# An encoder block on one core: gate weights' loads, the squares and 1/rms of h2, and the loads of the last activations

## The chip, the cores and the metric

The kernel runs on one core of a Trainium2 chip. The metric is the device time of one execution in microseconds (us); lower is better. Five engines work side by side, each with a queue of its own that it works through in order: TensorE (PE in the profile; its weight loads PEld) does the matrix products, VectorE (DVE) and ScalarE (ACT) the elementwise work, GpSimd (POOL) some elementwise work and DMAs that add to what is there, SyncE (SP) issues most DMAs. The three runs of the kernel before took 2572.34 to 2573.46 us, with a median of 2573.32 us.

## The reference

One layer of an encoder for 512 tokens of 2048 numbers each, all in float32:

```
u = rms_norm(h, mix_pre_g)
[q|k|v|conv_a|conv_b|gate_attn|gate_conv] = u @ w_in
y_attn = neighbourhood_attention(q, k, v, rpb) @ w_attn_o
y_conv = conformer_conv(conv_a, conv_b) @ w_conv_o
merged = sigmoid(gate_attn) * y_attn + sigmoid(gate_conv) * y_conv
h = h + rms_norm(merged @ w_out, mix_post_g)            # this is h2
u = rms_norm(h, ffn_pre_g)
f = (silu(u @ w_gate) * (u @ w_up)) @ w_down            # 5632 hidden units
h = h + rms_norm(f, ffn_post_g)
```

`rms_norm` divides every token by the root of the mean of its squares over the 2048 numbers and multiplies with a gain for each number.

## The kernel before

All tensors lie with the features on the 128 partitions and the 512 tokens in the free dimension, so that 2048 features are 16 tiles of 128x512 (`KT` = 16, `HT` = 8). Float32 precision is reached by splitting each operand into a rounded part and the rest (`split`, `wchunk`, tiles `..h` and `..l`, `whi` and `wlo`): a product of a 128x128 block of weights with a tile takes three matmuls. The rounded part is made on ScalarE, the rest on VectorE. The large products (the gates, the two FFN matrices) are done in a Strassen-like scheme of seven products (`strassen`, L219 and on).

Four pools matter. `slot` has 66 buffers of 128x512 and holds nearly everything. `raw` (five buffers of 128x1024) holds weights as they are loaded, `whi` and `wlo` (three each) their split parts. PSUM has four banks under `mm` (`bank`) and four under `at` (`abank`).

The order of the work on each engine is set when the program is built: a planner takes the instructions by their place in the written order, gives out buffers as they come free, and lets a later instruction go ahead of an earlier one that is not ready by its own estimate of times. `keep_in_program_order` (a pin) makes an instruction wait for its place in the written order on its engine. `load_in_order` is a pinned load on SP's queue. On the chip each engine then follows its fixed order and waits for semaphores.

The stages are: the input norm and the convolution branch; v; q and k with the attention, head by head; the gates; the two output projections of the branches; `w_out`, and h2; the FFN's first matrix (gate and up), and its second (`w_dn`); the last norm. The change touches four places.

**The first gate products (L546 to L595).** Eight chunks of gate weights (`raw[c]`, from `w_gg`) and eight pairs of tiles of the normalized input (`uf[c]`, from `u_d`), which are turned into the Strassen operands, go through the same five `raw` buffers. The loads are issued in the order gate 0, un 0, gate 1, un 1, gate 2, un 2 and so on, all pinned, and are written ahead of the chunk's products.

**h2, its squares and 1/rms (L692 to L744).** Every tile of h2 is made on VectorE (`h2`, L698), split, written to `h_d`, and squared on ScalarE. The squares of the 16 tiles have to be added. Tiles 0, 1 and 2 start three sums (`acc`); the squares of tiles 3 to 13 are added to them by DMAs of GpSimd (L723), tile i to sum i % 3; tiles 14 and 15 stay by themselves. `folded` (L328) then adds these five tiles up on VectorE (L331), `rstd` (L291) sums over the partitions with short matmuls against a column of ones (L299, two passes for each block of 128 tokens: eight instructions for one tile), and VectorE and GpSimd make 1/rms of it. `by_column` (L312) spreads it over the partitions with matmuls (L316), and r3 is copied from there (L734). The steps are put between products that do not need them: the `gemm` at L729 has four chunks, and calls one of the functions in `between` behind each. 1/rms stands behind the second, r3 behind the third. With r3 the FFN's first products are finished (L740 to L744), and all operands of the next stage are made (L754 and on).

**The loads of the last activations (L870 to L908).** The second FFN matrix is done in three parts: four tiles of the hidden units, 16 tiles by the Strassen scheme, in pairs of outputs `o` = 0, 2, .. 14, and the last 24 (`acts`, tiles 20 to 43). `load` (L791) fetches a tile with a pinned DMA on GpSimd's queue and splits it (tiles `fa..`). The first three (`EARLY`) are written ahead of the pair `o` = 14 and five more (`MORE`) behind its products. Behind every pair but the last, `added` (L866) multiplies the pair's two outputs on GpSimd and adds them to `y_d` with a DMA, all pinned.

**The last norm (L915 to L975).** The last two outputs (14 and 15) are made in two halves of 256 tokens, A and B, so that the first half's norm can be made while the second half's products run. The squares of outputs 0 to 13 are summed in `acc[0]`; `sq` holds those of 14 and 15. In half A both are added to `acc[0]` on VectorE (L331), in half B only output 14's, and output 15's goes into `rstd` as a second tile. The half's 1/rms stands behind the first chunk of half B.

## Time and profile before

| | |
|---|---|
| median of three runs | 2573.32 us |
| the profiled execution | 2572.55 us |
| its span, from the first to the last instruction | 2570.8 us |
| granted TensorE clock, mean | 0.992 |
| busy: TensorE, VectorE, ScalarE, GpSimd | 98%, 73%, 44%, 13% |
| waits of TensorE over 2 us in total, by line | 8 |

The profile lists for every engine what it executed and, from the semaphores, what ended each wait. "PE f L195 <- DVE u_15l L704: 2.3, 1, 2.3" reads: TensorE, at line 195, waited once, for 2.3 us, until VectorE had written `u_15l` at line 704. In a timeline the columns are start, duration, engine, line, operation and tiles, and in brackets the idle time ahead of the instruction and what ended it. In a table of stretches the columns are the length, the busy time of TensorE, its weight loads, VectorE, ScalarE and GpSimd (with the number of instructions), the granted TensorE clock as a share, the busy share of the DMA engines, and GB/s. Durations of neighbouring matmuls overlap.

### The profile page before, as it was taken

What the parts mean: (1) busy time and instruction counts of PE and PEld (TensorE: products, weight loads), DVE (VectorE), ACT (ScalarE), POOL (GpSimd) and SP (SyncE); (2) the same over time, 40 slices, a digit from 0 to 9 for tenths busy, and PEclk for the clock granted to TensorE, in tenths of its full rate; (3) what the DMA queues carried; (4) which work ended last, traced back from release to release, by engine and by line L of the source; (5) the groups of instructions that cost most, each with busy time, mean ns of one, the idle gap of its engine ahead of it and who ended that gap; (6) DMA issues with size and microseconds to landing.
All of it is one profiled execution on the core that took longest, in us unless ns stands there. A gap on an engine that the chain in (4) does not pass through costs nothing.

```text
span 2570.8 us, 34587 instructions
## 1 busy us (share of the span) xinstructions
PE 2517.5 (98%) x13187; PEld 2160.3 (84%) x13187; DVE 1867.3 (73%) x2406; ACT 1123.7 (44%) x1652; POOL 338.4 (13%) x384
## 2 busy tenths in 40 slices
PE   9999999999999999999999999999999999989996
PEld 7888888788888888888888888888888878878886
DVE  5999896587776664337888888788888888863335
ACT  5223333455554422225455555555555564442221
POOL 0110222210000021001001111112110102240002
PEclk9999999999999999999999999999999999999998
DMA  6246323486667445237256566666665667773334
GB/s 208 94 146 194 109 93 108 142 267 185 191 195 245 137 136 185 95 113 208 96 159 181 172 166 186 189 197 194 211 202 172 183 243 183 182 246 109 110 113 156
DMA packets 144053, 430.57 MB, mean 167 GB/s; under 512 B 16912, under 2 KB 24208, under 8 KB 143888
## 3 DMA queue, kind: packets, MB, share of 16 engines
q1 hardware_dynamic: 102144, 324.32, 38.3%
q0 software_dynamic: 22160, 69.48, 12.9%
q10 hardware_dynamic: 19584, 34.58, 3.6%
q8 instruction: 103, 1.69, 0.3%
q14 instruction: 62, 0.51, 0.1%
HBM read 371.95 MB, written 49.28 MB: 164 GB/s over the span
## 4 chain that ended last, share of the span: by engine, by line
PE 82%; DVE 10%; issue 4%; DMA 2%; ACT 1%; POOL 1%; ACTq 0%; DVEq 0%; SPq 0%; POOLq 0%
PE f L251 19%; PE f L253 10%; PE g L251 7%; PE g L253 4%; PE pd L181 3%; PE pd L177 3%; PE pd L180 3%; DVE cv L397 3%; PE d L251 3%; PE qk L181 2%; PE qk L180 2%; PE qk L177 2%; PE po L181 2%; PE po L180 2%; PE po L177 2%
## 5 line engine op out<-in xcount | busy, mean ns | idle before, releaser
L397 DVE SCALAR_TENSOR_TENSOR cv<-z,vec,cv 128x497 f32<-128x497 f32 (+14 forms) x240 | 190.9, 797 | 4.8
L132 DVE TENSOR_TENSOR wlo_wd<-raw_wd,whi_wd 128x1024 fp32r<-128x1024 f32 (+1 forms) x58 | 64.2, 1111 | 110.3 <-ACT whi_wd L131 109.0
L131 ACT CAST whi_wd<-raw_wd 128x1024 fp32r<-128x1024 f32 (+1 forms) x58 | 54.0, 934 | 166.8 <-PE pd L180 120.0
L132 DVE TENSOR_TENSOR wlo_wo<-raw_wo,whi_wo 128x1024 fp32r<-128x1024 f32 x36 | 47.5, 1319 | 106.6 <-ACT whi_wo L131 106.4
L131 ACT CAST whi_wo<-raw_wo 128x1024 fp32r<-128x1024 f32 x36 | 37.9, 1054 | 130.0 <-PE po L180 122.6
L309 POOL TENSOR_TENSOR r_r<-r_v,mhalf 128x2 f32<-128x2 f32 (+1 forms) x6 | 7.0, 1174 | 504.9 <-DVE r_v L307 454.6
L131 ACT CAST whi_y<-raw_y 128x1024 fp32r<-128x1024 f32 x32 | 33.5, 1052 | 79.4 <-PE py L180 76.2
L131 ACT CAST whi_qk<-raw_qk 128x1024 fp32r<-128x1024 f32 x32 | 33.6, 1051 | 77.1 <-PE qk L180 56.5
L132 DVE TENSOR_TENSOR wlo_qk<-raw_qk,whi_qk 128x1024 fp32r<-128x1024 f32 x32 | 40.5, 1264 | 32.2 <-ACT whi_qk L131 32.0
L132 DVE TENSOR_TENSOR wlo_y<-raw_y,whi_y 128x1024 fp32r<-128x1024 f32 x32 | 53.3, 1668 | 10.8 <-ACT whi_y L131 9.6
L650 DVE TENSOR_TENSOR gg<-py,gg 128x512 f32<-128x512 f32 x32 | 21.8, 690 | 52.6 <-PE py L181 52.6
L780 POOL TENSOR_TENSOR asum<-asum,asq 128x512 f32<-128x512 f32 x15 | 19.2, 1283 | 241.6 <-ACT asq L779 241.6
L177 PE MATMUL py<-ycl,whi_y 128*128 128x512 f32 x128 | 49.8, 389 | 0.0
L180 PE MATMUL py<-ych,whi_y 128*128 128x512 f32 x128 | 49.8, 389 | 0.0
L181 PE MATMUL py<-ych,wlo_y 128*128 128x512 f32 x128 | 49.8, 389 | 0.0
L823 ACT ACTIVATE sg<-sg 128x512 f32<-128x512 f32 x39 | 24.8, 635 | 52.2 <-DVE sg L289 52.2
L478 POOL TENSOR_TENSOR bm<-braw,msk 128x128 f32<-128x128 f32 x56 | 40.7, 760 | 16.3 <-DMA braw<-in_rpb 16.2
L804 POOL TENSOR_TENSOR an<-an,asum 128x512 f32<-128x512 f32 x16 | 26.5, 1655 | 103.6 <-DMA an<-a_d 101.7
L911 DVE TENSOR_TENSOR y<-pd,y 128x512 f32<-128x512 f32 x14 | 9.7, 692 | 41.6 <-PE pd L181 38.8
L159 PE MATMUL f<-b,whi_f 128*128 128x256 f32 x128 | 36.7, 287 | 2.2 <-DVE b L154 2.2
L868 POOL TENSOR_TENSOR ys<-ys,irow 128x512 f32<-128x512 f32 x16 | 27.1, 1692 | 77.3 <-PE d L251 41.4
L160 PE MATMUL f<-b,whi_f 128*128 128x256 f32 x128 | 36.2, 283 | 0.0
(3079 smaller groups left out, 8496.7 us busy)
## 6 DMA issues: line engine op xcount, KB each, us to landing
raw_wd<-in_w_dn SPq DMA_DIRECT2D x42, 512.0 KB, 3.7
raw_wo<-in_w_out SPq DMA_DIRECT2D x36, 512.0 KB, 3.9
raw_qk<-in_w_qk SPq DMA_DIRECT2D x32, 512.0 KB, 3.7
a_d<-sg ACTq DMA_DIRECT2D x44, 256.0 KB, 3.7
raw_v<-in_w_v SPq DMA_DIRECT2D x16, 512.0 KB, 4.5
raw_y<-in_w_ao SPq DMA_DIRECT2D x16, 512.0 KB, 4.2
gg<-g_d SPq DMA_DIRECT2D x32, 256.0 KB, 4.3
raw_y<-in_w_co SPq DMA_DIRECT2D x16, 512.0 KB, 3.6
```

What stands on the lines that cost most here:

```text
L131: cast(hi[:, s], raw[:, s])
L132: nc.vector.tensor_tensor(out=lo[:, s], in0=raw[:, s], in1=hi[:, s].bitcast(F32), op=ALU.subtract)
L159: nc.tensor.matmul(o, hi, t[:, B], start=first, stop=False, skip_group_check=True)
L160: nc.tensor.matmul(o, hi, t[:, A], start=False, stop=False, skip_group_check=True)
L177: mmul = nc.tensor.matmul(ps, hi[:, s], al, start=first, stop=False)
L180: nc.tensor.matmul(ps, hi[:, s], ah, start=False, stop=False)
L181: nc.tensor.matmul(ps, lo[:, s], ah, start=False, stop=last)
L251: nc.tensor.matmul(ps, hi[:, ws[k]], t, start=first and k == 0, stop=False, skip_group_check=True)
L253: nc.tensor.matmul(ps[:, A], lo[:, ws[k]], t[:, A], start=False, stop=last and k == HT - 1, skip_group_check=True)
L397: nc.vector.scalar_tensor_tensor(out=a[:, to], in0=z[:, fr], scalar=col(C_WDW, i * CW + w), in1=a[:, to], op0=ALU.mult, op1=ALU.add)
L478: nc.gpsimd.tensor_tensor(out=bm[:, o + i - i0], in0=raw[:, :, i * BC : (i + 1) * BC], in1=msk[:, o + i - i0, None, :].broadcast_to([P, RO ...
L868: tc.keep_in_program_order(nc.gpsimd.tensor_tensor(out=t, in0=t, in1=irow, op=ALU.mult))
```

## The change

Four places are changed.

1. The loads of the gate weights are no longer pinned, and the loads for later chunks are written behind the products of a chunk instead of ahead of them. The loads of `u_d` stay pinned.
2. The squares of h2 are added in two chains of DMAs (tiles 0 and 1, to which tiles 2 to 11 are added), and the last four (12 to 15) on VectorE as they come. `rstd` now reads three tiles and is called behind the first chunk of the `gemm`, r3 behind the second.
3. The first three of the last activations are loaded ahead of the pair `o` = 12 instead of 14.
4. In the last norm, output 15's squares of half A are no longer added to `acc[0]`; `rstd` reads them as a second tile in both halves.

```
@@ gates
     def load_gate(c):
         raw.append(wraw(f"g0_{c}"))
-        load_in_order(raw[c], w_gg[c])
+        nc.sync.dma_start(raw[c], w_gg[c])
...
     load_gate(0)
     load_un(0)
-    load_gate(1)
     for c in range(HT):
-        if c + 1 < HT:
-            load_un(c + 1)
-        if c + 2 < HT:
-            load_gate(c + 2)
         hi, lo = wchunk(w_gg[c], f"g0_{c}", raw=raw[c])
...
+        if c == 0:
+            load_gate(1)
+        if c + 1 < HT:
+            load_un(c + 1)
+        if c + 2 < HT:
+            load_gate(c + 2)
@@ h2
                 sq = slot(f"h{i}_sq")
                 nc.scalar.activation(sq, f[i], AF.Square)
-                if 3 <= i < KT - 2:
-                    nc.gpsimd.dma_start(acc[i % 3], sq, accum_op=ALU.add)
+                if i in (0, 1, KT - 4):
+                    acc.append(sq)
+                elif i < KT - 4:
+                    nc.gpsimd.dma_start(acc[i % 2], sq, accum_op=ALU.add)
                 else:
-                    acc.append(sq)
+                    folded([acc[2], sq])
...
         between=(
-            lambda: None,
-            lambda: r.append(rstd(folded(acc), D, "r3", pin=True)),
+            lambda: r.append(rstd(acc, D, "r3", pin=True)),
             lambda: nc.scalar.copy(r3, by_column(r[0], "r3", pin=True)),
@@ last activations
     for o in range(0, KT, 2):
-        if o == KT - 2:
+        if o == KT - 4:
             acts = [load(DN_S + k) for k in range(EARLY)]
@@ last norm
-            if n == 0 or q is sq[0]:
+            if q is sq[0]:
                 folded([acc[0], q], cols)
...
-            lambda: r.append(rstd(acc + sq[1:] * n, D, f"r4{n}", blocks, pin)),
+            lambda: r.append(rstd(acc + sq[1:], D, f"r4{n}", blocks, pin)),
```

## The prediction

> **What bounds the kernel now.** I read the page's first part, then TensorE's own list of waits.

> ```profile
> span 2570.8 us, 34587 instructions
> PE 2517.5 (98%) x13187; PEld 2160.3 (84%) x13187; DVE 1867.3 (73%) x2406; ACT 1123.7 (44%) x1652; POOL 338.4 (13%) x384
> ```
> ```profile
> PE r_s L299 <- DVE y_sq L331: 3.5, 1, 3.5
> PE d L251 <- ACT d14v L241: 3.4, 1, 3.4
> PE pt L518 <- DVE sc L509: 2.8, 3, 1.4
> PE f L251 <- ACT f5h L246: 2.4, 1, 2.4
> PE f L195 <- DVE u_15l L704: 2.3, 1, 2.3
> ...
> PE pd L177 <- DVE fa29l L142: 2.1, 1, 2.1
> ```

> TensorE is busy for 98% of the span, so only its few idle places can be won: 2570.8 − 2517.5 = 53.3 us, the output's tail among them. The columns of the second list are total us, times, longest us. Each part of the change has one or two of these waits beside it: `pt` stands ahead of the gate products, `u_15l` and `f5h` stand on the two sides of 1/rms of h2, `d14v` and `fa29l` go with the loads of the activations, and `r_s` at 3.5 us is the last 1/rms.

> An idle place costs more than its own length, as the granted clock shows in stretches cut to the clock's own steps:

> ```profile
> 480.86:489.71 8.85, 3.86 (x24) 3.28 (x25) 6.07 (x18) 3.89 (x11) 0.00 (x0) 1.00 0.00 0
> 489.71:493.12 3.41, 3.32 (x13) 2.92 (x12) 2.71 (x4) 1.92 (x4) 0.00 (x0) 0.50 0.00 0
> 1209.92:1213.34 3.42, 1.92 (x9) 1.26 (x7) 1.28 (x2) 0.00 (x0) 0.00 (x0) 1.00 0.05 16
> 1295.26:1302.08 6.82, 5.60 (x17) 4.83 (x18) 4.55 (x5) 4.11 (x5) 0.00 (x0) 0.50 0.71 246
> 2261.23:2268.05 6.82, 5.51 (x17) 4.74 (x18) 3.12 (x4) 4.10 (x6) 2.30 (x5) 0.50 0.99 384
> ```

> After the length of a stretch stands TensorE's busy time, and the clock is the third number from the end. The clock is 0.50 for 6.82 us after the `f5h` wait and again after the `d14v` wait, 3.4 us of work lost each time, and for 3.41 us (1.7 lost) ahead of the gate products, where TensorE had been idle for 8.85 − 3.86 = 5.0 us. A stretch with 1.92 of 3.42 us busy (third row) left it at 1.00. [...]

> **Gate weights' loads.** The four products' loads change their place in the written order and lose their pin; each `un` load stays pinned.

> ```profile
> 437.06 0.33 SPq L91 DMA_DIRECT2D raw_g<-in_w_gg  x1
> ```
> ```profile
> 480.89 0.59 ACT L141 CAST qk_1h<-qk 128x512 fp32r<-128x512 f32 x1 [10.29 <-PE qk L181]
> ...
> 490.60 1.05 ACT L131 CAST whi_g<-raw_g 128x1024 fp32r<-128x1024 f32 x1
> ```

> The first gate weights are asked for at 437.06 and cast only at 490.60, although ScalarE sat idle for 10.29 us before 480.89. The cast's place in ScalarE's queue, behind the last head's softmax, keeps TensorE without other products there; the load's landing does not. The queue gives its five buffers in the written order, and that order (gate 0, un 0, gate 1, un 1, gate 2) is the same after the change. I take 0. If the planner now places the cast ahead of the softmax, the 5.0 us ahead of the gate products and the lower clock's 1.7 go: a gain of up to 6.7. If a gate load comes late instead, I bound the loss by the longest wait of the list, 3.5. Nothing new is queued behind a load on SP: an `un` load still follows the gate load written ahead of it.

> **Squares and 1/rms of h2.** Eleven accumulating DMAs in three chains become ten in two chains (tiles 2 to 11); tiles 13 to 15 are added on VectorE. The four additions at the end go, three earlier ones come.

> ```profile
> L723 POOL DMA_DIRECT2D h_sq<-h_sq x11: 866/866/923, 1178.0 to 1201.3; - x11
> ...
> DMA to landing us min/median/max: 3.4/6.9/10.6
> ```
> ```profile
> 1212.03 1.42 DVE L331 TENSOR_TENSOR h_sq<-h_sq 128x512 f32<-128x512 f32 x2 [7.06 <-DMA h_sq<-h_sq]
> 1213.36 0.74 DVE L704 SCALAR_TENSOR_TENSOR u_15l<-f,vec,u_15h 128x512 fp32r<-128x512 f32 x1
> ```

> The first row has the accumulations' first and last issue, 1178.0 and 1201.3, the second the least, median and longest time to landing; the last one lands 10.6 us after its issue. VectorE's additions wait 7.06 us for it with `u_15l` queued behind them, and TensorE waits 2.3 us for `u_15l`. With the last tiles on VectorE no addition waits for a DMA. Three additions of 0.7 us (two take 1.42) ahead of `u_15l` are 2.1 us, against the 7.06 us of standing idle: TensorE's 2.3 us go.

> ```profile
> 1222.01 0.39 PE L177 MATMUL f<-u_0l,whi_f 128*128 128x512 f32 x1
> ...
> 1227.45 0.95 PE L299 MATMUL r_s<-ones,h_sq 128*128 128x1 f32 x8
> ...
> 1233.84 1.05 PE L316 MATMUL r_b<-ident,r_r 128*128 128x128 f32 x8
> ```
> ```profile
> 1234.93 0.59 ACT L734 COPY r<-r_b 128x512 f32<-128x512 f32 x1
> ```
> ```profile
> 1250.00:1300.00 50.00, 45.45 (x342) 43.10 (x341) 49.74 (x111) 29.18 (x66) 0.00 (x0) 0.95 0.25 79
> ```

> The sums (`r_s`) move from behind the second chunk of products (1227.45) to behind the first (1222.01), the rows (`r_b`) from behind the third to behind the second. The sums read three tiles instead of one: 24 short products for 8, 16 × 0.12 = 1.9 us more. So the first chunk ends at 1222.0 − 2.3 = 1219.7, the sums at 1222.6, the second chunk, 1227.45 − 1222.01 = 5.4 us long, at 1228.0: `r_b` comes 5.8 us ahead of 1233.84. What follows hangs on it. VectorE is busy for 49.74 of the 50 us from 1250 on, the work that starts from r3's copy at 1234.93; TensorE's `f5h` wait ends this stretch. All of it starts 5.8 us earlier, VectorE being idle before. TensorE can follow: it saves 2.3 and pays 1.9 ahead of it, and within it the waits shrink. I take −5.8. The lower clock at 1295 lasts two steps; a smaller wait should leave one of them, −1.7. Bounds: none of the move is kept (only 1.9 − 2.3 = −0.4), or it and the whole lower clock, −9.2.

> **Activations by another pair.** Loads 20 to 22 are written ahead of pair 12 instead of pair 14, on POOL's queue behind `added` of pair 10 instead of pair 12.

> ```profile
> 2235.54 0.87 POOL L869 DMA_DIRECT2D y_d<-ys  x1 [0.30 <-POOL ys L868]
> ...
> 2255.65 4.62 POOL L793 DMA_DIRECT2D ad<-a_d  x8
> ```
> ```profile
> 2235.89 1.05 ACT L246 CAST d12h<-d12q 128x1024 fp32r<-128x1024 f32 x1 [1.25 <-PE d L251]
> 2238.22 0.59 ACT L241 COPY d12v<-d 128x512 f32<-128x512 f32 x1 [1.28 <-DVE d L272]
> ...
> 2261.38 0.62 ACT L141 CAST fa20h<-ad 128x512 fp32r<-128x512 f32 x1 [4.89 <-DMA ad<-a_d]
> 2261.91 0.58 ACT L241 COPY d14v<-d 128x512 f32<-128x512 f32 x1
> ```

> The eight loads leave POOL at 2255.65, after `added` of pair 12, and the first lands 5.7 us later; its cast `fa20h` was put ahead of the copy `d14v` in ScalarE's queue, so the copy is late and TensorE waits 3.4 us. One pair earlier POOL is free at 2236.1 (its write of 2235.54 is the last of `added` of pair 10) and the load lands at about 2241.8; if the planner puts the cast at the same point of the pair, it stands ahead of `d12v` (2238.22) and that copy is 4 us late in the same way. The other five loads still leave after pair 12. So I do not count the 3.4 us as won: one such stall stays, here or there, for 0. What is won is behind it. Three activations fewer are loaded, cast and subtracted when the last products begin, and the 2.1 us for `fa29l` fall away. I take −2.1. Bounds: both pairs stall, +3.4 and its half clock +3.4; or neither does, −6.8 and −2.1.

> **The last 1/rms.** The addition of tile 15's left half goes, and `r_s` reads two tiles.

> ```profile
> 2539.95 0.42 ACT L927 ACTIVATE sq<-y 128x256 f32<-128x256 f32 x1 [1.31 <-DVE y_sq L331]
> ```
> ```profile
> 2540.40 0.43 DVE L331 TENSOR_TENSOR y_sq<-y_sq,sq 128x256 f32<-128x256 f32 x1 [0.48 <-ACT sq L927]
> ```

> The 3.5 us wait ends with this chain: square, then addition of 0.43 us. The square itself waits for the addition before it. Without the last link `r_s` starts 0.43 us earlier; four more short products, 4 × 0.12, can run ahead of that square. I take −0.4, with 0 and −0.9 as bounds. The square's late place remains, and with it 3 us of the wait.

> **Sum.** 0 − 5.8 − 1.7 − 2.1 − 0.4 = −10.0 us. The profiled execution took 2572.55 us, 1.75 more than its span, and the median of the three runs, 2573.32, is 0.8 above it: 2573.3 − 10.0 = 2563.3.

> **The rivals.** (1) Queues are planned anew and more waits go: the gate cast moves ahead (−6.7) or the pairs do not stall at all (−6.8). For it: both waits come from an order in ScalarE's queue, not from a missing engine. Against it: the loads' written order hardly changes. Either of them gives about 2556.6, both 2549.8. (2) The activation stall doubles: `fa20h` ahead of `d12v` and `fa23h` ahead of `d14v`. For it: the repeating pairs and unchanged `added`. Against it: fewer loads stand together. 2563.3 + 6.8 = 2570.1. (3) The new place of `r_s` is too early, and the kernel becomes slower. Two chains of five accumulations each run one after the other. From 1178.0 on, at 6.9 us each they end at 1212.5, 7 us ahead of 1219.7; at the longest 10.6 us they end at 1231. The point of decision is (1219.7 − 1178) / 5 = 8.3 us. At 10.6, TensorE stands for 11.3 us with the pinned `r_s` at its head and the second chunk, `r_b` and the next stage's products behind it; `r_b` then starts at 1231 + 2.9 + 5.4 = 1239.3, 5.5 us later than before, all VectorE work behind it as well, and the half clock after such a wait adds up to 3.4. With the other parts' −2.5: 2573.3 + 5.5 + 3.4 − 2.5 = 2579.7. For it: the DMA time grows with the crowd around 1200. Against it: fewer accumulations are in flight at once, and the crowd ends at 1212. (4) The move of 1/rms brings no more than the 0.4 us, because VectorE's planned order does not use it; the other terms remain: 2573.3 − 0.4 − 2.5 = 2570.4. For it: that order is made from estimates; against it, VectorE's idle time ahead of the copy. (5) The lower clock at 1295 is not tied to the waits ahead of it and lasts its two steps after the change too: 2563.3 + 1.7 = 2565.0. Against it, each of the three stretches at 0.50 follows a place of idle TensorE. [...]

> **How the numbers follow.** My forecast 0.40 (own range 2558 to 2567), rival 1 0.20, rival 2 0.14, rival 3 0.12, rival 4 0.09, rival 5 0.05. A measurement of this kernel tells about 0.2%, 5.1 us, from no change. Faster by more: the forecast, rivals 1 and 5 and a small share (0.02) of 2: 0.67. Within: nearly all else of 2 and 4, 0.20. Slower: rival 3 with a little for an unforeseen order, 0.13. The range goes down to 2552, between rival 1's one and two gains, and up to 2575, past rivals 2 and 4, leaving out rival 3 and the deepest gains.

> **What would show it.** Right: no wait of `u_15l`; `r_s` of h2 with 24 rows behind the first chunk and `r_b` about 6 us earlier; a shorter `f5h` wait and one step of lower clock there; `fa29l` under 1 us; a wait of about 3 us for `d12v` or `d14v`. Wrong: TensorE waiting at `r_s` for a DMA; `f5h` as late as before relative to the end of the products; both `d12v` and `d14v` waiting, or neither; `whi_g` cast before 481 us.

## The result, and the profile after

The changed kernel takes 2558.69 us (median of four runs, 2554.56 to 2561.35), the kernel before, beside it, 2572.83 us (2570.04 to 2573.46): 14.1 us less. The ratio is 0.9946, with a 95% interval of 0.9928 to 0.9963. The profiled execution took 2559.14 us. The head of its page:

```profile
span 2557.4 us, 34634 instructions
PE 2514.0 (98%) x13207; PEld 2158.8 (84%) x13207; DVE 1866.0 (73%) x2404; ACT 1122.6 (44%) x1652; POOL 342.5 (13%) x383
```

TensorE's own list of waits (total us, times, longest us) has changed at every place that the prediction spoke of:

```profile
PE g L570 <- DVE wlo_g L132: 5.8, 1, 5.8
PE d L251 <- ACT d12v L241: 3.3, 1, 3.3
PE g L251 <- ACT g2h L246: 2.8, 1, 2.8
PE f L251 <- ACT f5h L246: 1.6, 1, 1.6
...
PE pd L177 <- DVE fa30l L142: 1.5, 1, 1.5
...
PE r_s L299 <- ACT sq L929: 1.0, 1, 1.0
...
PE d L251 <- ACT d14v L241: 0.7, 1, 0.7
```

Gone are the waits for `u_15l` and for the last `r_s` (3.5 us); `f5h` is down from 2.4 to 1.6. New are 5.8 and 2.8 us at the gates, and 3.3 us for `d12v` stands where 3.4 for `d14v` stood.

Where the time went is read best from the starts of the same product in the two traces (us from the span's start):

| start of | before | after | lag |
|---|---|---|---|
| first gate product (`un0l`) | 493.01 | 480.54 | −12.5 |
| first product with `g2h` | 536.62 | 537.68 | +1.1 |
| first `py` (attention's output projection) | 810.75 | 816.08 | +5.3 |
| first FFN product (`u_0h`) | 1167.20 | 1172.73 | +5.5 |
| `r_s` of h2 | 1227.45 | 1224.87 | −2.6 |
| first product with `f6h` | 1315.89 | 1313.68 | −2.2 |
| first `pd` (four tiles of hidden units) | 2062.67 | 2060.45 | −2.2 |
| first product with `d0h` | 2113.76 | 2108.24 | −5.5 |
| first product with `d12h` | 2231.05 | 2225.54 | −5.5 |
| first product with `d14h` | 2250.61 | 2251.49 | +0.9 |
| first product of the last two outputs (`pl`) | 2509.01 | 2504.07 | −4.9 |
| end of the span | 2570.78 | 2557.36 | −13.4 |

So the gates lose about 5.5 us, h2 and its 1/rms win 5.5 + 2.2 = 7.7, the first part of `w_dn` wins 3.3, the activations' loads bring next to nothing, and the last norm wins 13.4 − 4.9 = 8.5.

**The gates.** Stretches of the changed kernel, cut to the clock's steps (length, busy time of TensorE, its weight loads, VectorE, ScalarE, GpSimd; then granted clock, DMA share, GB/s):

```profile
480.52:489.17 8.65, 8.65 (x44) 7.17 (x43) 6.55 (x17) 4.72 (x10) 0.00 (x0) 1.00 0.19 61
519.89:523.30 3.41, 0.00 (x0) 0.00 (x0) 3.41 (x11) 2.02 (x5) 3.41 (x7) 1.00 0.92 311
523.30:530.13 6.83, 5.62 (x13) 4.45 (x14) 6.52 (x14) 2.49 (x7) 2.86 (x6) 0.50 0.97 331
543.78:547.19 3.41, 0.92 (x4) 0.79 (x5) 1.64 (x2) 2.97 (x5) 0.00 (x0) 1.00 1.02 396
2233.38:2236.79 3.41, 0.70 (x6) 0.50 (x5) 0.40 (x1) 0.54 (x2) 0.00 (x0) 1.00 0.89 299
2236.79:2243.62 6.83, 6.22 (x19) 5.25 (x20) 4.94 (x7) 3.56 (x6) 0.00 (x0) 0.50 0.28 90
```

The first row is the last head's softmax: TensorE is now busy throughout, with gate products, where it had stood for 5.0 us. The second and third show the price: a window with nothing to do, then 6.83 us at half clock. The fourth is the wait for `g2h`, and the last two belong to `d12v`. What came late is seen on SP's queue, first in the changed kernel, then in the kernel before (start, us, the load):

```profile
491.13 0.33 SPq L264 DMA_DIRECT2D g2s<-in_w_cg  x1
491.52 0.42 SPq L264 DMA_DIRECT2D g3s<-in_w_cg  x1
496.24 0.38 SPq L91 DMA_DIRECT2D un<-u_d  x1
498.63 0.33 SPq L553 DMA_DIRECT2D raw_g<-in_w_gg  x1
500.31 0.38 SPq L91 DMA_DIRECT2D un<-u_d  x1
509.89 0.33 SPq L553 DMA_DIRECT2D raw_g<-in_w_gg  x1
```
```profile
504.12 0.33 SPq L91 DMA_DIRECT2D raw_g<-in_w_gg  x1
505.83 0.38 SPq L91 DMA_DIRECT2D un<-u_d  x1
506.26 0.55 SPq L264 DMA_DIRECT2D g2s<-in_w_cg  x1
```

The weights of the next stage, `g2s` and `g3s`, now go ahead of the fifth `un` and of the gate chunks 5 to 7. Before, the first of them left behind the sixth `un`. The delay reaches TensorE through two other queues: ScalarE's casts waited 14.1 us in all for gate weights to land (4.8 before), and VectorE waited behind ScalarE. So the seventh chunk's `wlo_g` ran only at 523.24, though its `whi_g` was cast at 516.55: VectorE first worked through its overdue Strassen operands.

**h2.** TensorE's timeline in the changed kernel (start, duration, engine, line, operation, tiles, count):

```profile
1219.43 0.39 PE L177 MATMUL f<-u_0l,whi_f 128*128 128x512 f32 x1
...
1224.87 2.73 PE L299 MATMUL r_s<-ones,h_sq 128*128 128x1 f32 x24
...
1233.05 1.05 PE L316 MATMUL r_b<-ident,r_r 128*128 128x128 f32 x8
```

`r_s` stands behind the first chunk, with 24 instructions and no wait ahead of it. Counted from the first FFN product, `r_b` starts after 1233.05 − 1172.73 = 60.3 us; before, it was 1233.84 − 1167.20 = 66.6.

**The activations.** ScalarE in pair 12 of the changed kernel; the brackets hold the idle time and what ended it:

```profile
2236.25 0.62 ACT L141 CAST fa20h<-ad 128x512 fp32r<-128x512 f32 x1 [4.82 <-DMA ad<-a_d]
2236.77 0.58 ACT L241 COPY d12v<-d 128x512 f32<-128x512 f32 x1
```

It is the picture of pair 14 before, one pair earlier: a cast that waits for its load, with the copy that TensorE needs behind it.

**The last norm.** The two passes of `r_s` for half A in the changed kernel:

```profile
2524.22 0.50 PE L299 MATMUL r_s<-ones,y_sq 128*128 128x1 f32 x4
2525.98 0.50 PE L299 MATMUL r_s<-ones,sq 128*128 128x1 f32 x4
```

They start 20 us after the first `pl`, with no wait; before, `r_s` came 32 us after it, at 2540.88.

### The profile page after: what moved, and what is told of

Same layout as the page of the kernel before. It is cut to its first block, busy times and chain, and to the rows that moved or that the text cites. A ratio compares the mean times of both kernels' runs of the same rounds, so it can differ in the third digit from the quotient of the medians.

```text
span 2557.4 us, 34634 instructions
## 1 busy us (share of the span) xinstructions
PE 2514.0 (98%) x13207; PEld 2158.8 (84%) x13207; DVE 1866.0 (73%) x2404; ACT 1122.6 (44%) x1652; POOL 342.5 (13%) x383
## 3 DMA queue, kind: packets, MB, share of 16 engines
q8 instruction: 103, 1.69, 0.3%
## 4 chain that ended last, share of the span: by engine, by line
PE 83%; DVE 9%; issue 4%; DMA 2%; ACT 1%; POOL 1%; ACTq 0%; DVEq 0%; SPq 0%; POOLq 0%
PE f L251 19%; PE f L253 10%; PE g L251 7%; PE g L253 4%; PE pd L181 3%; PE pd L177 3%; PE pd L180 3%; PE d L251 3%; DVE cv L397 3%; PE qk L181 2%; PE qk L180 2%; PE qk L177 2%; PE po L181 2%; PE po L180 2%; PE po L177 2%
## 5 line engine op out<-in xcount | busy, mean ns | idle before, releaser
L131 ACT CAST whi_wd<-raw_wd 128x1024 fp32r<-128x1024 f32 (+1 forms) x58 | 54.0, 934 | 166.0 <-PE pd L180 121.6
L131 ACT CAST whi_wo<-raw_wo 128x1024 fp32r<-128x1024 f32 x36 | 37.9, 1054 | 130.0 <-PE po L180 122.7
L131 ACT CAST whi_y<-raw_y 128x1024 fp32r<-128x1024 f32 x32 | 33.5, 1051 | 79.4 <-PE py L180 75.3
L131 ACT CAST whi_qk<-raw_qk 128x1024 fp32r<-128x1024 f32 x32 | 33.7, 1052 | 77.1 <-PE qk L180 56.5
L132 DVE TENSOR_TENSOR wlo_y<-raw_y,whi_y 128x1024 fp32r<-128x1024 f32 x32 | 53.3, 1668 | 10.8 <-ACT whi_y L131 9.8
L177 PE MATMUL py<-ycl,whi_y 128*128 128x512 f32 x128 | 49.8, 389 | 0.0
L181 PE MATMUL py<-ych,wlo_y 128*128 128x512 f32 x128 | 49.8, 389 | 0.0
```

The source lines that it names most:

```text
L131: cast(hi[:, s], raw[:, s])
L132: nc.vector.tensor_tensor(out=lo[:, s], in0=raw[:, s], in1=hi[:, s].bitcast(F32), op=ALU.subtract)
L177: mmul = nc.tensor.matmul(ps, hi[:, s], al, start=first, stop=False)
L181: nc.tensor.matmul(ps, lo[:, s], ah, start=False, stop=last)
```

## The experiments

Twelve kernels were run, four at a time in the order of the table, each group beside the kernel before (medians 2572.89, 2572.05 and 2572.57 us). A difference to the kernel before is taken within its group; one to the changed kernel's 2558.69 us runs across groups. Medians and ratios with 95% intervals:

| kernel | us | ratio to before |
|---|---|---|
| part 1 alone (a_only) | 2575.76 | 1.0014 (1.0003 to 1.0025) |
| part 2 alone (b_only) | 2565.36 | 0.9971 (0.9960 to 0.9982) |
| part 3 alone (c_only) | 2572.41 | 0.9997 (0.9989 to 1.0006) |
| part 4 alone (d_only) | 2562.96 | 0.9959 (0.9947 to 0.9971) |
| parts 2, 3, 4 (no_a) | 2555.85 | 0.9929 (0.9916 to 0.9941) |
| changed, `g2s` and `g3s` held back (after_pin_g2s) | 2552.08 | 0.9919 (0.9904 to 0.9934) |
| before, a buffer for output 15's squares (d_slot) | 2562.16 | 0.9953 (0.9940 to 0.9965) |
| changed, activations fetched earlier (after_early_fetch) | 2551.40 | 0.9919 (0.9905 to 0.9932) |
| changed, both of these edits (both_fixes) | 2547.44 | 0.9900 (0.9887 to 0.9914) |
| gate loads unpinned alone (a_unpin) | 2576.66 | 1.0016 (1.0008 to 1.0025) |
| h2: squares alone (b_squares) | 2571.17 | 0.9994 (0.9985 to 1.0003) |
| h2: earlier 1/rms alone (b_move) | 2566.32 | 0.9972 (0.9962 to 0.9982) |

The changed kernel's interval, 0.9928 to 0.9963, still overlaps those of after_pin_g2s and after_early_fetch by a little; both_fixes lies clear of it.

### One part at a time

My theory was that the four parts act in places of their own and add up; the rival, that the planner's new order ties them together.

Part 1 (a_only):

```
-        load_in_order(raw[c], w_gg[c])
+        nc.sync.dma_start(raw[c], w_gg[c])
...
```

and the calls of `load_gate` and `load_un` behind a chunk's products, as in part 1.

> The kernel before with part 1 alone (gate loads unpinned and written behind the products). Theory: this part costs time by itself; in the changed kernel TensorE's lag against the kernel before grows by 5.5 us between the last attention head and the first product with w_gate (first f<-u_0l at 1172.73 instead of 1167.20). So about 2572.8 + 5.5 = 2578.3 us, with g waiting about 5.9 us for wlo_g near 518 us and about 2.8 us for g2h near 543 us, and two stretches at half clock behind them. Rival (the parts act only together, since the order of the work is planned anew): within 2 us of the kernel before, and those two waits are not there.

It is 2.9 us slower. The two waits are there without the other parts:

```profile
PE g L570 <- DVE wlo_g L132: 4.4, 1, 4.4
...
PE g L251 <- ACT g2h L246: 2.9, 1, 2.9
```

So the loss belongs to this part, though it is half of the 5.5 us that the two profiles gave.

Part 2 (b_only):

```
-                if 3 <= i < KT - 2:
-                    nc.gpsimd.dma_start(acc[i % 3], sq, accum_op=ALU.add)
+                if i in (0, 1, KT - 4):
+                    acc.append(sq)
+                elif i < KT - 4:
+                    nc.gpsimd.dma_start(acc[i % 2], sq, accum_op=ALU.add)
                 else:
-                    acc.append(sq)
+                    folded([acc[2], sq])
...
-            lambda: None,
-            lambda: r.append(rstd(folded(acc), D, "r3", pin=True)),
+            lambda: r.append(rstd(acc, D, "r3", pin=True)),
```

> The kernel before with part 2 alone (two chains, last tiles on VectorE, 1/rms one chunk earlier). Theory: it wins what the two traces show between the first product with w_gate and the first f6 product, 7.7 us (lag from +5.53 to -2.20), by itself: 2572.8 - 7.7 = 2565.1 us, without the u_15l wait and with no lower clock near 1295 us. If the 3.3 us that are won around the first part of w_dn (lag -2.22 to -5.51) are a consequence of this part, 2561.8. Rival: the gain needs the rest, and the f5h wait with its lower clock stays: 2570 to 2573.

7.5 us faster. By the medians, the 3.3 us around the first part of `w_dn` did not come on top.

Part 3 (c_only):

```
-        if o == KT - 2:
+        if o == KT - 4:
             acts = [load(DN_S + k) for k in range(EARLY)]
```

> The kernel before with part 3 alone (activations loaded by another pair). Theory (the stall moves): one wait of about 3.3 us for d12v with half a clock behind it in place of the one for d14v, so the time stays within 1.5 us of the kernel before, 2571.3 to 2574.3. If the 3.3 us around the first part of w_dn come from this part, 2569.5. Rival (both pairs stall): about 2579.6.

No difference that can be measured. TensorE's wait for `d12v` is 3.0 us, that for `d14v` 1.2 (2.7 to 3.4 in the kernels that load there): the stall has moved.

Part 4 (d_only):

```
-            if n == 0 or q is sq[0]:
+            if q is sq[0]:
...
-            lambda: r.append(rstd(acc + sq[1:] * n, D, f"r4{n}", blocks, pin)),
+            lambda: r.append(rstd(acc + sq[1:], D, f"r4{n}", blocks, pin)),
```

> The kernel before with part 4 alone (output 15's squares of half A not folded, read by r_s as a second tile). Theory: the one addition that goes frees the order at the end: r_s no longer waits 3.5 us for the squares, no lower clock follows, and r_s of half A stands ahead of the last chunk's products: the two traces differ by 8.5 us between the first product of the last part and the end (lag -4.94 to -13.43), so 2572.8 - 8.5 = 2564.3 us. Rival, the sum of the prediction: only one addition of 0.43 us is saved, 2572.4, and the order at the end of the changed kernel comes from the other parts.

9.9 us faster, the largest gain of the four. ScalarE's square of output 15 and the two passes of `r_s` in this kernel:

```profile
2528.61 0.41 ACT L927 ACTIVATE sq<-y 128x256 f32<-128x256 f32 x1
```
```profile
2527.54 0.50 PE L299 MATMUL r_s<-ones,y_sq 128*128 128x1 f32 x4
...
2529.30 0.50 PE L299 MATMUL r_s<-ones,sq 128*128 128x1 f32 x4
```

In the kernel before that square ran at 2539.95, behind output 14's addition of half B.

The four singles add up to 2.9 − 7.5 − 0.5 − 9.9 = −15.0 us, against −14.1 for the whole change. The other way round, part 1 taken away from the whole (no_a, which loads the gates as before):

```
+        load_in_order(raw[c], w_gg[c])
-        nc.sync.dma_start(raw[c], w_gg[c])
...
```

> The changed kernel without part 1 (parts 2, 3 and 4 on the kernel before). Theory (the parts act in places of their own and add up): 2572.9 - 7.5 - 0.5 - 9.9 = 2555.0 us from the three single runs, so faster than the changed kernel, and no wait for wlo_g or g2h over 1 us between 500 and 560 us. Rival (the planner's new order makes the parts depend on each other): off from 2555 by more than 3 us.

2555.85 us, 0.9 us from that sum. Against the kernel before of its own group it is 16.2 us faster, 1.7 less than the three singles' 17.9; both lie within the 3 us. Its interval overlaps that of the changed kernel, so this run alone would not show that part 1 costs time; a_only and a_unpin do.

The 3.3 us around the first part of `w_dn` (first `pd` to first `d0h`) are tied to no part of the change. This stage took 51.1 us in the profile before and 47.8 in the profile after; in the profiles of a_only, b_only, c_only and d_only it took 48.5, 48.4, 49.2 and 48.4, in a_unpin 50.7, in b_squares 47.7. The longest wait there for `wlo_wd` is between 0.6 and 2.7 us over all the profiles, and the profile before had met a long one with a half clock behind it. It is a row of TensorE's list that the prediction does not show:

```profile
PE pd L181 <- DVE wlo_wd L132: 3.1, 2, 2.5
```

Why that wait varies stays open.

### Part 1: the pin or the place

Unpinned, but written where the loads were (a_unpin):

```
-        load_in_order(raw[c], w_gg[c])
+        nc.sync.dma_start(raw[c], w_gg[c])
```

> The kernel before with the gate loads unpinned, but written where they were, ahead of the products. Theory (the lost pin is what acts, not the new place in the written order): the same as part 1 alone, 2575.8 us, 0 to 6 us over the kernel before, with the gate products begun near 480.6 us and the waits for wlo_g of about 4 to 6 us near 518 us and for g2h of about 3 us near 542 us. Rival (the place acts): the kernel before, 2572, with the gate products begun near 493 us.

4.1 us slower, with the gate products begun early (482.45) and the same two waits:

```profile
PE g L575 <- DVE wlo_g L132: 5.0, 1, 5.0
PE g L251 <- ACT g2h L246: 4.3, 2, 3.3
```

On SP's queue `g2s` (493.06) and `g3s` (493.45) again go ahead of the fifth `un` (498.13). The lost pin acts; the place in the written order is not needed for it.

Then the changed kernel with the two overtaking loads held back (after_pin_g2s), in `strassen`:

```
-        nc.sync.dma_start(s1, w1[:, :1024])
+        (load_in_order if name in ("g2", "g3") else nc.sync.dma_start)(s1, w1[:, :1024])
```

> The changed kernel with the first loads of the Strassen weights g2s and g3s pinned, so that they stay behind all gate and un loads on SP's queue. Theory: part 1 loses because these two loads, each with an accumulating load behind it, overtake un4 and the later gate chunks and take the DMA engines from them; held back, the waits for wlo_g (5.9 us) and g2h go and the early start of the gate products is kept: 2558.7 less 5.9 and the half clock behind it (up to 3.4), so 2549 to 2553. Rival (the stage is bound by the DMA engines whatever the order, or the late g2s makes the Strassen products wait instead): the wait moves to the first products with g2h, 2556 us or more.

6.6 us faster than the changed kernel by the medians (20.0 below the kernel before of its group, against 14.1). The early start is kept, the wait for `wlo_g` is down to 1.3 us, and the first product with `g2h` starts at 530.66 instead of 537.68. The wait for `g2h` stays, so the rival had its share: 3.0 us remain there. Its profile also shows something that the edit does not aim at, both pairs waiting:

```profile
PE d L251 <- ACT d14v L241: 3.2, 1, 3.2
...
PE d L251 <- ACT d12v L241: 2.6, 1, 2.6
```

The cast `fa23h` stood ahead of `d14v` and waited 5.51 us for its load, where in the changed kernel it waited 3.06. Why the load came later here stays open.

### Part 2: the squares or the place of 1/rms

The squares as in part 2, with three tiles in `r_s`, but `r_s` and `r_b` where they were (b_squares):

```
-            lambda: r.append(rstd(folded(acc), D, "r3", pin=True)),
+            lambda: r.append(rstd(acc, D, "r3", pin=True)),
...
```

> The kernel before with the first half of part 2: two chains, the last four squares on VectorE, three tiles in r_s, but r_s and r_b where they were, behind the second and the third chunk. Theory (the gain of part 2 is the earlier 1/rms): the wait for u_15l (2.3 us) goes, 16 more short products (1.9 us) come, the f5h wait of 2.4 us with its half clock stays: 2571 to 2573 us. Rival (it is the addition's wait for the DMA that costs): 2565 to 2568, most of what part 2 brings.

And the old squares with `r_s` one chunk earlier (b_move):

```
-            lambda: None,
             lambda: r.append(rstd(folded(acc), D, "r3", pin=True)),
```

> The kernel before with the second half of part 2: three chains and the five tiles folded as before, but r_s behind the first chunk and r_b behind the second. Theory: r_b comes one chunk, 5.4 us, earlier, the f5h wait shrinks from 2.4 to about 1.6 us, and the u_15l wait stays: most of part 2's 7.5 us, so 2566 to 2568. If the additions at the end come too late for the earlier place, TensorE waits at r_s for them and the gain is smaller by that wait. Rival (the squares carry the gain): 2571 to 2573.

1.4 us (within the uncertainty) and 6.3 us faster: the earlier 1/rms carries the gain. The waits for `f5h`, first of b_squares, then of b_move:

```profile
PE f L251 <- ACT f5h L246: 2.4, 1, 2.4
```
```profile
PE f L251 <- ACT f5h L246: 1.6, 1, 1.6
```

The wait goes with the place of `r_b`, not with the additions.

### Part 3: what stalls the pair

Loads ahead of pair 10, casts written behind pair 12 (after_early_fetch); `fetch` is the buffer and the DMA of `load`, without its `split`:

```
-        if o == KT - 4:
-            acts = [load(DN_S + k) for k in range(EARLY)]
+        if o == KT - 6:
+            ads = [fetch(DN_S + k) for k in range(EARLY)]
         w0, w1 = ...
         c11, c12, c21, c22 = strassen(...)
+        if o == KT - 4:
+            acts = [split(t, f"fa{DN_S + k}") for k, t in enumerate(ads)]
```

> The changed kernel with the first three activations loaded one pair earlier still (ahead of pair 10), but split behind the products of pair 12, so that their casts stand among pair 12's copies long after the loads have landed. Theory (the stall is a cast that stands in ScalarE's queue ahead of a copy and waits for its load): the 3.3 us wait for d12v goes, and with it the half clock behind it where there is one: 2558.7 - 3.3 = 2555.4, down to 2552. Rival (the wait for d12v is not tied to the casts, for instance the crowd on the DMA engines in that pair): 2558.7 with a wait of about 3 us for a d12v or d10v copy.

7.3 us faster than the changed kernel by the medians (20.7 below the kernel before of its group, against 14.1). ScalarE now finds the tile there:

```profile
2223.69 0.62 ACT L141 CAST fa20h<-ad 128x512 fp32r<-128x512 f32 x1
...
2226.74 0.58 ACT L241 COPY d12v<-d 128x512 f32<-128x512 f32 x1
```

No idle time stands ahead of the cast, and there is no wait for `d12v` of 0.5 us or more. More is won than the 3.3 us wait because the half clock behind it (6.83 us in the changed kernel's profile) goes too: from the first product with `d12h` to the first with `d14h` it is 19.94 us instead of 25.95, 6.0 less. Not all of the difference between the two profiles is the edit's: 2.3 us had already been won at the gates, which it does not touch, where this execution waited 4.1 us for `wlo_g` instead of 5.8 and met one step of half clock fewer.

### Part 4: the addition or the buffer

The kernel before with one line changed (d_slot); `arow` is a row of the stage before, no longer read:

```
-    sq = [slot(f"sq{o}") for o in (KT - 2, KT - 1)]
+    sq = [slot(f"sq{KT - 2}"), arow]
```

> The kernel before with one edit: the squares of output 15 lie in a buffer of their own (the one that held the row arow, no longer in use) instead of one of the 66 slots; all additions stay as they are. Theory (slots): with 48 tiles of the activations, 16 of y, the sum and the squares of 14, all 66 slots are taken, so the first square of output 15 waits for the slot of output 14's squares, and with it r_s; with a buffer of its own r_s of half A goes in time though its addition is still made, and the gain of part 4 appears without part 4: about 2563 us, no wait of 3.5 us at r_s. Rival (the addition that part 4 drops, or the second tile in r_s, is what frees the order): 2572.9 us and the same wait.

The gain of part 4 without part 4: 9.9 us. ScalarE's squares of outputs 14 and 15 and TensorE's `r_s`:

```profile
2523.48 0.41 ACT L927 ACTIVATE sq<-y 128x256 f32<-128x256 f32 x1
2526.40 0.41 ACT L927 ACTIVATE asum<-y 128x256 f32<-128x256 f32 x1
```
```profile
2528.20 0.55 PE L299 MATMUL r_s<-ones,y_sq 128*128 128x1 f32 x4
```

`asum` is the buffer of `arow`. With it the square follows output 14's by 2.9 us, all additions are made, and `r_s` does not wait. The addition never was the cost; the missing slot was.

### Both remedies together

The edits of after_pin_g2s and after_early_fetch in one kernel (both_fixes):

```
+        (load_in_order if name in ("g2", "g3") else nc.sync.dma_start)(s1, w1[:, :1024])
...
+        if o == KT - 6:
+            ads = [fetch(DN_S + k) for k in range(EARLY)]
```

> The changed kernel with both edits together: g2s and g3s pinned behind the gate and un loads, and the first three activations loaded ahead of pair 10 and split behind pair 12. Theory (the two stalls have nothing to do with each other): 2558.7 - 6.6 - 7.3 = 2544.8 us by the medians of the two single edits, 2547 by their profiled executions, with neither a wait for wlo_g over 2 us nor one for d12v. Rival (part of those gains was a matter of which execution was met, since the half clock behind a wait comes in some and not in others): 2549 to 2552.

2547.44 us (2545.27 to 2549.26), the fastest of all: 25.1 us below the kernel before of its group, and 11 below the changed kernel. The longest waits of TensorE are now

```profile
PE g L251 <- ACT g2h L246: 3.1, 1, 3.1
PE f L251 <- ACT f5h L246: 1.6, 1, 1.6
```

It lies between theory and rival: 2.6 us above the sum of the medians, on the sum of the profiled executions.

## Why the prediction was right or wrong

The direction and the size came out near: 2558.7 measured, 2563.3 forecast, −14.1 against −10.0. Only one of the four terms (h2) was right in mechanism and size, so the near total is in good part luck.

| step | forecast | alone | bounds given |
|---|---|---|---|
| gate loads | 0 | +2.9 | −6.7 to +3.5 |
| h2's squares and 1/rms | −5.8 − 1.7 | −7.5 | −0.4 to −9.2 |
| activations | −2.1 | −0.5 | −8.9 to +6.8 |
| last 1/rms | −0.4 | −9.9 | −0.9 to 0 |

**Gate loads: wrong.** The step that failed is "that order (gate 0, un 0, gate 1, un 1, gate 2) is the same after the change", taken as if it settled the queue. That order did stay. What changed is who else may stand in the queue: the pins had kept `g2s` behind `un` 5, and `g3s` behind `un` 6. "Nothing new is queued behind a load on SP" looked at the `gate` and `un` loads alone. The part of rival 1 in which the cast moves ahead came true, and the first gate cast now runs at 469.67 instead of 490.60; but what it won (5.0 us of standing and 1.7 of half clock; 3.4 of half clock in the profiles of the seven other kernels with pinned gate loads) was given back with 5.8 and 2.8 us of waiting further on. The mark "`whi_g` cast before 481 us" was met, as one of those that would show me wrong.

**h2: right, by the mechanism named.** No wait for `u_15l`, 24 instructions in `r_s`, `r_b` 6.3 us earlier (5.8 forecast), a shorter `f5h` wait. At 1295 us there was no step of lower clock at all, where one was forecast. That is no accident of one execution: all seven profiled kernels with the 2.4 us wait for `f5h` have a half clock there, and none of the seven with 1.6 us, so rival 5 is refuted. b_move shows that the gain is the move's. Rival 3 did not come: TensorE did not wait at `r_s` for a chain of DMAs. Rival 4 is refuted. What the working left out: in the profiles of b_only, b_squares and no_a a step at 0.50 follows the 24 short products (below).

**Activations: the move was right, its gain was not seen.** The stall went from pair 14 to pair 12, for 0 as forecast. Of what lay behind it, `fa29l` no longer waits 2.1 us, but `fa30l` waits 1.5 in its place, so the −2.1 was at most 0.7 and no run resolves it; "`fa29l` under 1 us" was the wrong mark. The half clock behind the stall lasted 6.83 us in the profiles before and after, but none follows the wait for `d12v` in those of c_only and no_a, so no fixed price can be put on it. Rival 2 did not come in the changed kernel, where `d14v` costs 0.7 us, nor in c_only and no_a (1.2 and 1.0); in after_pin_g2s, with the same loads, both pairs did wait. It is not refuted as a mechanism.

**Last 1/rms: right in sign, wrong in cause and 9.5 us too small.** The failing sentence is "The square itself waits for the addition before it", which I read as an order that stays: "The square's late place remains, and with it 3 us of the wait". The wait was for a buffer. At that point 48 tiles of activations, 16 of y, the sum and output 14's squares hold 66 slots, all there are, and output 15's squares took the slot that output 14's gave back. The square does not read what that addition writes, and this should have made me ask for the buffer. It cost more than its 3.5 us, since the whole half A's norm was pushed behind half B's products, with the half clock at 2541 (3.41 us at 0.50). Which tile's slot the square takes in d_only the trace does not say; that a slot is what it lacked is shown by d_slot.

The range held by luck, because a gain of 9.5 us that was not seen outweighed a loss of 2.9 that was not seen, and 1.6 of a gain that did not come.

## What to carry to other kernels

When an instruction waits for an operation whose result it does not read, look for the buffer that this operation gives back: another buffer for one small tile was worth as much here as the best part of the change, 9.9 us each. Before a pin is taken away, list what may overtake in that queue, not only the pinned loads among themselves. And look for casts that wait for a load with work for TensorE behind them in their queue: here `fa20h` waited 4.82 us for its load, with the copy `d12v` behind it. Moving load and cast together moved TensorE's stall (3.4 us for `d14v` before, 3.3 for `d12v` after); moving the loads ahead of the casts removed it (no wait for `d12v` of 0.5 us or more in after_early_fetch).

## What the runs showed of the hardware

```profile
1211.96:1215.37 3.41, 1.42 (x7) 0.84 (x5) 1.45 (x3) 0.00 (x0) 0.00 (x0) 1.00 0.03 9
1215.37:1222.20 6.83, 6.17 (x15) 4.82 (x16) 4.59 (x6) 1.04 (x1) 0.00 (x0) 0.50 0.37 106
```

Before, the same wait (2.3 us against 2.6) fell across two steps with 1.92 and 2.59 us busy, and the clock stayed at 1.00. So the wait cost its 2.3 us there, and in c_only about 6.0 by my estimate: 2.6, and half of the 6.83 us at 0.50 behind it. The steps lie elsewhere in each execution, and the half clock seen behind one wait in one profile did not come in the other; the one behind `f5h` came in all seven kernels with the 2.4 us wait.

The four steps with 1.69 us or more busy that half clock followed hold products of one column. One, in b_move from 860.04 us, has eight of them (in the convolution branch) and a wait of 1.05 us. The other three (b_only, b_squares, no_a) hold 22 to 24 of the 24 of h2's `r_s`, as in b_only:

```profile
1221.94:1225.35 3.41, 3.41 (x28) 3.27 (x28) 0.80 (x2) 0.85 (x1) 0.55 (x1) 1.00 0.02 5
1225.35:1228.76 3.41, 3.41 (x9) 2.68 (x9) 0.50 (x1) 0.00 (x0) 1.40 (x1) 0.50 0.48 154
```

TensorE is busy throughout the first stretch by its records, and the clock falls all the same. In these three steps the short products take 2.36 to 2.57 us; in the four other kernels with the 24 they fall into two steps, none holds more than 2.03 us of them (1.58 and 1.15 in the changed kernel), and no half clock follows. That the short products bring it is not shown: no run varied their number alone.
